# An encoder block on one core: another order of its opening, low parts of four output weights on another engine, and one pair of loads ahead of another

## The chip, the cores and the metric

The kernel runs on one NeuronCore of a Trainium2 chip. The metric is the device time of one execution in microseconds (us). Five engines work beside each other, each through its own list of instructions, in order: PE (TensorE: matrix products and transposes), DVE (VectorE), ACT (ScalarE), POOL (GpSimd) and SP (SyncE, which here only issues DMAs). They wait for each other through semaphores.

## The reference, cut to what matters

All tensors are float32; 1024 tokens, 1024 features.

```
h = LN_in(x)
p = h @ W_in                      # 1024 x 11776: q/k/v of 3 dilated attention groups,
                                  # HGRN2 query, two forget gates, input, output gate, two merge gates
a = dilated_attention(p)          # 512 wide
r = bidirectional_HGRN2(p)        # 1024 wide
m = sigmoid(g_a) * (a @ W_a) + sigmoid(g_r) * (r @ W_r)
h = LN1(alpha * h + m @ W_o)
h = LN2(alpha * h + SwiGLU(h))    # W_ffn_in 1024 x 5632, W_ffn_out 2816 x 1024
```

## The kernel before, in words

Every large matrix product keeps float32 precision by splitting both operands: a high part `hi` is a rounded copy (a cast on ACT), the low part `lo = x - hi` is a subtraction, and each product is three matmuls, hi*hi, hi*lo and lo*hi (`mm3`). `split` (L202) makes such a pair; its last argument says whether POOL or DVE subtracts.

On top of that the products of W_in and W_ffn_in are Strassen-Winograd products of a two by two block scheme: seven products take the place of eight. For W_in the activations are cut into two halves of 512 tokens (tiles 0 to 3, tiles 4 to 7 of 128 tokens) and two halves of 512 features. The blocks are called b11 (features 0 to 511 of the first four tiles), b21 (features 512 to 1023 of the same), b12 and b22 (the same of the last four tiles). The right operands of the seven products are b11, b21, b22 and the four sums t1 = b12 - b11, t2 = b22 - t1, t3 = b22 - b12 and t4 = b21 - t2 (before forms t4 as b21 - b11 - t3, the same thing). They are kept, as hi and lo, in `xb`. The left operands are blocks of weights a11, a12, a21, a22 and their sums s1 to s4. `ORDER = (1, 2, 6, 5, 7, 3, 4)` is the order of the products: product 1 uses b11, 2 uses b21, 6 uses t2, 5 uses t1, 7 uses t3, 3 uses b22, 4 uses t4. One product is twelve 128x512 matmuls.

`phase0` (L306) makes `xb`: for each tile of 128 tokens it loads x, takes mean and variance on DVE, normalises on ACT, stores the normalised tile to DRAM (`ah_d`, for the residual later), transposes on PE (`transposed`, L280), scales and shifts the transposed pieces out of PSUM on ACT or DVE, and splits them. Tiles are taken whole, one after the other.

`stream` (L473) is a generator that does W_in's products: groups `n` of four 128-wide column tiles, two pairs `g` in a group, and for each group the seven products for both pairs. It loads the weight blocks (`block`, L460), splits each three products ahead (`prep`), and passes each result to an evacuation on ACT or DVE. `phase1` runs it; attention and HGRN2 units run beside it as generators, on PE in between and on the other engines, and near the end `residual` (L364) loads the normalised tiles back, scales them with alpha and stores them for LN1.

`phase2` does W_a, W_r and W_o. W_o is held whole as hi and lo in two halves, `wo[0]` and `wo[1]` (`wo1hi`, `wo1lo` in the trace), made of eight chunks of 128 columns by `wo_chunk` (L1166) from two staging buffers. It ends with LN1, the blocks b11 to t4 of the next scheme, of which b22, t3 and t4 go to DRAM (`td`). `ffn_in` loads those back (`t_raw`, L1471), in the order b22, t3, t4, while the first products of W_ffn_in run; `ffn_raws` (L1405) loads the next weights. `ffn_out` and LN2 end the kernel.

Instructions are put in order per engine by a scheduler that follows the order of writing and priorities; `ordered` and `behind` add an order between two instructions, without a semaphore where they are on one engine.

Of the kernel before, what the change touches and what calls it, by code (L numbers as in the profile page):

```python
# [10 lines left out]
F32 = mybir.dt.float32  # L11
# [63 lines left out]
CST_PAD = 160  # L75
# [4 lines left out]
class Block:  # L80
    evac_ahead = 1000

    def __init__(self, ctx, tc, x, ln_in_g, ln_in_b, w_in, hgrn_lb, hgrn_norm_g, w_att_up, w_hgrn_up,
# [28 lines left out]
        self.ah_d = scratch("ah", 8)  # L112
# [25 lines left out]
    def consts(self):  # L138
# [20 lines left out]
        self.my = take(64).bitcast(I32)  # L159
        self.mhalf = cst.tile([128, 8], F32, name="mhalf")  # L160
        nc.vector.memset(self.mhalf, -0.5)

    def columns(self, pool):

        nc = self.nc
        rows = pool.tile([128, 128], F32, name="vrows")
        at, r = {}, 0
        for name, src, n in (("gin", self.ln["in"][0], 8), ("bin", self.ln["in"][1], 8), ("g1", self.ln["1"][0], 8),
                             ("b1", self.ln["1"][1], 8), ("lb", self.lbw, 32), ("ng", self.ng, 1)):
            nc.scalar.dma_start(rows[r:r + n, :], bass.AP(tensor=src.tensor, offset=src.offset, ap=[[128, n], [1, 128]]))  # L170
            at[name] = r
            r += n
        ps = self.ps_sd()
        nc.tensor.transpose(ps[:, :r], rows[:r, :], self.ident[:r, :r])
        a, b = self.cst.tile([128, 32], F32, name="vc"), self.cst1.tile([128, 33], F32, name="vc1")
        nc.vector.tensor_copy(a, ps[:, 0:32])
        nc.vector.tensor_copy(b, ps[:, 32:65])
        self.col = {n: a[:, at[n]:at[n] + 8] for n in ("gin", "bin", "g1", "b1")}
        self.lbraw, self.ngraw = b[:, 0:32], b[:, 32:33]

# [21 lines left out]
    def split(self, hi, lo, src, eng_hi="act", eng_lo="pool", key=None):  # L202
        nc = self.nc
        if eng_hi == "act":
            nc.scalar.copy(hi, src)  # L205
        else:
            nc.vector.tensor_copy(hi, src)
        e = nc.gpsimd if eng_lo == "pool" else nc.vector
        ins = e.tensor_sub(lo, src, hi.bitcast(F32))  # L209
        if key:  # L210
            self.ordered(key, ins)

# [14 lines left out]
    def behind(self, ins):  # L227

        if self.gone is not None:
            self.tc.add_manual_dep(ins.ins, self.gone, mybir.DependencyInfo(  # L230
                mybir.DependencyClass.NoSync, mybir.DependencyReason.DATA), reason="order behind an evacuation")
# [21 lines left out]
    def mm3(self, ps, whi, wlo, xhi, xlo, first, last, **kw):  # L253
# [3 lines left out]
        nc.tensor.matmul(ps, wlo, xhi, start=False, stop=last, **kw)  # L257
# [22 lines left out]
    def transposed(self, pool, n, q, g, b, v=None, bufs=2, on_act=(1, 3, 6)):  # L280

        nc = self.nc
        ps = self.ps_sd()
        for k in range(4):
            nc.tensor.transpose(ps[:, 128 * k:128 * (k + 1)], n[:, 128 * (4 * q + k):128 * (4 * q + k + 1)],
                                self.ident)
        if v is None:
            v = pool.tile([128, 4, 128], F32, name="tsv", tag="tsv", bufs=bufs)
        for k in range(4):
            kk = 4 * q + k  # L290
            p = ps[:, 128 * k:128 * (k + 1)]
# [6 lines left out]
    def phase0(self, pool):  # L298


        nc, kept, rest = self.nc, [], []

        def hold(n):
            t = pool.tile([128, D], F32, name=n, tag="xt", bufs=7)
            return t, [t[:, HALF * i:HALF * (i + 1)].rearrange("p (k c) -> p k c", k=4) for i in range(2)]

        xs = []

        def load():
            tt = len(xs)  # L310
            if tt < 8:
                xs.append(hold("xt"))
                for h in range(2 if tt == 0 else 1):
                    s = slice(HALF * h, HALF * (h + 1)) if tt == 0 else slice(0, D)
                    nc.sync.dma_start(xs[tt][0][:, s], self.x[128 * tt:128 * (tt + 1), s])

        for tt in range(8):
            for _ in range(4 if tt == 0 else 1):
                load()
            xt, (t1, t2) = xs[tt]  # L320
            if tt == 0:
                self.columns(pool)
                gc, bc = self.col["gin"], self.col["bin"]
            if tt == 1:
                self.rest()
            mv = self.stats(pool, xt, "0")
            self.normalise(pool, xt, xt, mv)
            nc.scalar.dma_start(self.ah_d[tt], xt)
            c = slice(128 * (tt % 4), 128 * (tt % 4) + 128)

            def put(name, v, c=c):
                hi, lo = self.xb[name]
                self.split(hi[:, :, c], lo[:, :, c], v, eng_lo="dve")

            if tt < 4:
                v = [self.half3("v11"), self.half3("v21") if tt == 0 else
                     pool.tile([128, 4, 128], F32, name=f"v21{tt}")]
                kept.append(v)
                for q, n in enumerate(("b11", "b21")):
                    self.transposed(pool, xt, q, gc, bc, v[q], on_act=(1, 3, 4, 6))  # L340
                    put(n, v[q])
                yield
                continue
            b11, b21 = kept[tt - 4]
            _, (b12, b22) = hold("vt")
            self.transposed(pool, xt, 0, gc, bc, b12, on_act=(0, 1, 3))
            nc.vector.tensor_sub(t1, b12, b11)
            put("t1", t1)
            self.transposed(pool, xt, 1, gc, bc, b22, on_act=(4, 5, 7))
            nc.vector.tensor_sub(t2, b22, t1)  # L350
            put("t2", t2)
            rest.append((put, b12, b22, b21, b11))

        for put, b12, b22, b21, b11 in rest:
            nc.vector.tensor_sub(b12, b22, b12)
            put("t3", b12)
        for put, b12, b22, b21, b11 in rest:
            put("b22", b22)
# [1384 lines left out]
```

## Time and profile before

| what | us |
|---|---|
| three runs: lowest, median, highest | 2112.54, 2115.25, 2120.56 |
| the profiled execution | 2111.09 |
| its span from first to last instruction | 2109.3 |
| PE busy in the span | 2022.3 |
| DVE, ACT, POOL busy | 1373.2, 925.0, 1087.2 |

PE is busy for 96% of the span, the others for half to two thirds. The span and what lies around it (1.8 us) make the profiled execution's time. In the listings below a row has start, duration, engine, source line, operation, output <- inputs, and in brackets the idle time before it with what ended it. Matmuls overlap, so the distance of two starts is what one of them costs, not its duration.

### The profile page before, as it was taken

To read this page: it belongs to the slowest core of one execution; us is meant where nothing else is said; L and a number is where in the kernel's file an instruction comes from. 1 tells how busy PE (TensorE), PEld (TensorE's weight loads), DVE (VectorE), ACT (ScalarE), POOL (GpSimd) and SP (SyncE) were. 2 spreads that over 40 slices of the span, in tenths; PEclk is the share of its full clock that TensorE was granted. 3 is DMA by queue.
4 is the path that set the end of the run, shared out by engine and by line. 5 is a ranking of instruction groups with operands and counts; after the bars stand their busy time and mean duration, and the time that the engine had idled before them with its cause. 6 is when DMAs were issued, how large, how long until landed. Compare 5 with 4: busy or idle time off the path is not lost.

```text
span 2109.3 us, 30917 instructions
## 1 busy us (share of the span) xinstructions
PE 2022.3 (96%) x10973; PEld 1673.1 (79%) x10973; DVE 1373.2 (65%) x2168; ACT 925.0 (44%) x1872; POOL 1087.2 (52%) x886
## 2 busy tenths in 40 slices
PE   4799999999999999999999999999999999999998
PEld 3678788888887888887888788788788888887876
DVE  7667745786459754788444823347867677767778
ACT  6544455444554435644355331144433333344542
POOL 3466654567446764565634864343666566630012
PEclk9899999999999999999999999999999999999999
DMA  5333442435333443343434764344434344348423
GB/s 204 110 129 100 138 159 93 142 129 168 121 105 126 135 154 120 125 131 115 157 117 143 279 222 142 98 136 134 155 120 147 129 148 136 113 161 296 160 90 125
DMA packets 273884, 301.10 MB, mean 143 GB/s; under 512 B 14081, under 2 KB 205378, under 8 KB 273730
## 3 DMA queue, kind: packets, MB, share of 16 engines
q1 hardware_dynamic: 266272, 273.73, 40.0%
q10 hardware_dynamic: 7458, 25.40, 3.1%
q8 instruction: 86, 1.41, 0.3%
q14 instruction: 68, 0.56, 0.1%
HBM read 200.25 MB, written 98.83 MB: 142 GB/s over the span
## 4 chain that ended last, share of the span: by engine, by line
PE 78%; DVE 10%; issue 5%; POOL 3%; DMA 2%; ACT 1%; SPq 0%; DVEq 0%; ACTq 0%; POOLq 0%
PE pj L255 17%; PE pj L256 17%; PE pj L257 17%; PE sd L255 6%; PE sd L256 6%; PE sd L257 6%; PE sd L1055 2%; POOL w_lo L209 2%; DVE qd L970 1%; DVE hR L1016 1%; DVE qd L973 1%; PE sd L811 1%; PE sd L860 1%; PE sd L887 1%; DVE hR L1015 1%
## 5 line engine op out<-in xcount | busy, mean ns | idle before, releaser
L209 POOL TENSOR_TENSOR w_lo<-wa,w_hi 128x512 fp32r<-128x512 f32 x276 | 382.2, 1392 | 301.0 <-ACT w_hi L205 271.0
L205 ACT CAST w_hi<-wa 128x512 fp32r<-128x512 f32 x276 | 170.0, 618 | 261.4 <-PE pj L256 169.3
L209 POOL TENSOR_TENSOR w_lo<-wsum,w_hi 128x512 fp32r<-128x512 f32 x88 | 128.7, 1472 | 112.7 <-PE sd L257 60.7
L200 POOL TENSOR_TENSOR mv<-mv,mhalf 128x1 f32<-128x1 f32 x24 | 15.4, 647 | 226.0 <-DVE mv L199 222.9
L209 POOL TENSOR_TENSOR w_lo<-f_raw,w_hi 128x512 fp32r<-128x512 f32 x66 | 102.0, 1554 | 55.8 <-ACT w_hi L205 54.6
L255 PE MATMUL pj<-xt1hi,w_hi 128*128 128x512 f32 x260 | 104.7, 403 | 17.4 <-ACT xt1hi L205 10.7
L205 ACT CAST w_hi<-wsum 128x512 fp32r<-128x512 f32 x88 | 54.8, 622 | 124.3 <-PE sd L256 114.8
L257 PE MATMUL pj<-xt1hi,w_lo 128*128 128x512 f32 x260 | 102.6, 395 | 1.0 <-POOL w_lo L209 1.0
L256 PE MATMUL pj<-xt1lo,w_hi 128*128 128x512 f32 x260 | 102.9, 396 | 0.0
L255 PE MATMUL pj<-xb22hi,w_hi 128*128 128x512 f32 x260 | 102.5, 394 | 0.0
L257 PE MATMUL pj<-xb22hi,w_lo 128*128 128x512 f32 x260 | 101.6, 391 | 0.0
L256 PE MATMUL pj<-xb22lo,w_hi 128*128 128x512 f32 x260 | 101.5, 390 | 0.0
L511 ACT COPY wkeep<-pj 128x512 f32<-128x512 f32 x138 | 80.1, 581 | 36.5 <-DVE evh L430 13.1
L209 POOL TENSOR_TENSOR w_lo<-ws,w_hi 128x512 fp32r<-128x512 f32 x46 | 64.5, 1406 | 60.9 <-ACT w_hi L205 58.8
L205 ACT CAST gwsum<-a_raw 128x512 fp32r<-128x512 f32 (+1 forms) x78 | 47.6, 615 | 100.2 <-PE pj L256 45.5
L403 DVE TENSOR_TENSOR evh<-wkeep,pj 128x512 f32<-128x512 f32 x66 | 57.6, 879 | 50.2 <-PE pj L257 35.4
L414 DVE TENSOR_TENSOR evh<-wkeep,pj 128x512 f32<-128x512 f32 x48 | 32.8, 683 | 88.0 <-PE pj L257 70.5
L489 POOL TENSOR_TENSOR wa<-wa,wa 128x512 f32<-128x512 f32 x46 | 68.2, 1492 | 31.8 <-DVE ws L488 29.8
L209 DVE TENSOR_TENSOR gwkeep<-a_raw,gwsum 128x512 fp32r<-128x512 f32 (+1 forms) x78 | 57.8, 742 | 40.5 <-ACT gwsum L205 37.6
L255 PE MATMUL pj<-xt2hi,w_hi 128*128 128x512 f32 x192 | 77.9, 407 | 2.6 <-ACT xt2hi L205 1.8
L255 PE MATMUL pj<-xb11hi,w_hi 128*128 128x512 f32 x192 | 77.4, 404 | 2.7 <-DVE evh L414 1.5
L257 PE MATMUL pj<-xt2hi,w_lo 128*128 128x512 f32 x192 | 76.0, 396 | 2.4 <-POOL w_lo L209 2.4
(407 smaller groups left out, 6572.2 us busy)
## 6 DMA issues: line engine op xcount, KB each, us to landing
wa<-in_w_in_dram SPq DMA_DIRECT2D x184, 256.0 KB, 3.2
f_raw<-in_w_ffn_in_dram SPq DMA_DIRECT2D x44, 512.0 KB, 4.1
a_raw<-gd SPq DMA_DIRECT2D x30, 512.0 KB, 3.7
gd<-fc SPq DMA_DIRECT2D x44, 256.0 KB, 2.0
gd<-fs SPq DMA_DIRECT2D x33, 256.0 KB, 2.1
tg<-evh SPq DMA_DIRECT2D x32, 256.0 KB, 3.3
tg<-tg SPq DMA_DIRECT2D x16, 512.0 KB, 3.5
y<-ahs SPq DMA_DIRECT2D x16, 512.0 KB, 4.7
```

The costliest lines, as they stand in the source:

```text
L205: nc.scalar.copy(hi, src)
L209: ins = e.tensor_sub(lo, src, hi.bitcast(F32))
L255: nc.tensor.matmul(ps, whi, xhi, start=first, stop=False, **kw)
L256: nc.tensor.matmul(ps, whi, xlo, start=False, stop=False, **kw)
L257: nc.tensor.matmul(ps, wlo, xhi, start=False, stop=last, **kw)
L403: self.left(nc.vector.tensor_tensor(o, self.order_src(add, g, kind), s, OP.add))
L414: self.left(nc.vector.tensor_add(t, add, ps))
L489: nc.gpsimd.tensor_sub(a["a21"], a["a11"], a["a21"])
L511: nc.scalar.copy(t, ps)
L811: nc.tensor.matmul(ps[:, tt % 2, :], q[pb, 128 * tt - 64:128 * tt + 64], k[pb, 128 * (tt - 1):128 * (tt + 1)], start=True, stop=True)
L860: nc.tensor.transpose(ps[:, o:o + 128], tile(tt, hd)[:, e:e + 128], ident)
L1055: nc.tensor.matmul(po[:, jj, :], l, r, start=(n == 0), stop=(n == len(terms) - 1))
```

## The change

Three places are edited; the functions for the near attention (`att_near`) are the same, line for line, in both kernels.

**The opening.** `phase0` first brings only b11 of tiles 0 to 3 to its end, then b21 of the same tiles, then tiles 4 to 7. The statistics' small steps go to POOL (an add, the power -0.5, and the shift) and stay in `mv0`; a half tile is normalised at a time; transposed pieces of a half tile leave PSUM on one engine, mostly, from one bank; t4 is b21 - t2 and t3 is subtracted on POOL. The normalised tile is no longer stored: `residual` loads x again and normalises it once more on ACT. The columns of parameters come in two parts, and loads are issued in a given order.

`stream` starts with product 1 of group 0 and group 1, then product 2 of both, and only then the other five of group 0, the other five of group 1, and all seven of each group that follows. Four explicit gates order casts and transposes behind others.

```
+        order = [(n, (p,)) for p in O[:2] for n in (0, 1)]
+        order += [(n, O[2:] if n < 2 else O) for n in range(len(tiles) // 4)]
...
+        def norm(tt, q):
+            x, mv = xs[tt][0][:, HALF * q:HALF * (q + 1)], self.mv0[:, tt, :]
+            ins = nc.scalar.activation(x, x, AF.Identity, bias=mv[:, 3:4], scale=mv[:, 2:3])
...
+        norm(3, 0)
+        turn(3, 0, v[3][0], (2, 3))
+        put(3, "b11", v[3][0])
+        self.gates = [at["hi", 1, "b11"]] * 2 + [at["hi", 3, "b11"]] * 2
+        run(2)
+        for tt in range(4):
+            if tt < 3:
+                norm(tt + 1, 1)
+            turn(tt, 1, v[tt][1], DVE if tt % 2 else ACT, self.product)
+            self.left(put(tt, "b21", v[tt][1]))
...
-            nc.sync.dma_start(a, self.ah_d[tt])
+            nc.sync.dma_start(a, self.x[128 * tt:128 * (tt + 1), :])
+            mv = self.mv0[:, tt, :]
+            nc.scalar.activation(a, a, AF.Identity, bias=mv[:, 3:4], scale=mv[:, 2:3])
```

On DVE this is what stands in the middle of the opening of the kernel before, while tiles 0 to 3 are made (`v_282` is tile 0's first half, `v_283` its second; `v_320` and `v_321` are tile 1's, `v_356` and `v_357` tile 2's, `v_392` tile 3's first).

```order
L295 TENSOR_SCALAR v_392<-sd,vc 128x128
L209 TENSOR_TENSOR xb21lo<-v_283,xb21hi 128x4x128
L488 TENSOR_TENSOR ws_690<-wa_428,wa_430 128x512
L360 TENSOR_TENSOR v_283<-v_283,v_282 128x512
L209 TENSOR_TENSOR xb11lo<-v_282,xb11hi 128x4x128
L295 TENSOR_SCALAR v_356<-sd,vc 128x128
L295 TENSOR_SCALAR v_357<-sd,vc 128x128
L209 TENSOR_TENSOR xb21lo<-v_321,xb21hi 128x4x128
L490 TENSOR_TENSOR wa_424<-ws_690,wa_424 128x512
```

Low parts of b11 and b21, sums of weights and differences for t4 stand mixed there. In the changed kernel the same engine has this, from the last low part of b11 on (`v_284`, `v_282`, `v_288`, `v_286` are the second halves of tiles 1, 0, 3, 2; `bn_453` and `bn_569` are the statistics of tiles 4 and 5):

```order
L220 TENSOR_TENSOR xb11lo<-v_287,xb11hi 128x4x128
L336 BN_STATS bn_453<-xt 128x6 x2
L336 BN_STATS bn_569<-xt 128x6 x2
L340 BN_AGGR mv_203<-bn_453 128x2
L340 BN_AGGR mv_203<-bn_569 128x2
L312 TENSOR_SCALAR v_284<-sd,vc 128x128 x4
L312 TENSOR_SCALAR v_288<-sd,vc 128x128 x4
L220 TENSOR_TENSOR xb21lo<-v_284,xb21hi 128x4x128
L220 TENSOR_TENSOR xb21lo<-v_282,xb21hi 128x4x128
L220 TENSOR_TENSOR xb21lo<-v_288,xb21hi 128x4x128
L605 TENSOR_TENSOR ws_504<-wa_273,wa_277 128x512
L605 TENSOR_TENSOR ws_529<-wa_275,wa_279 128x512
```

All of b11 is ahead of all of b21, and the statistics of the later tiles and the sums of weights have moved behind b11.

**Low parts of W_o's second half.** `wo_chunk` gets an argument, and chunks 4 to 7 are subtracted on DVE instead of POOL.

```
-    def wo_chunk(self, hl, c):
+    def wo_chunk(self, hl, c, by="pool"):
...
-        self.split(hi[:, :, s], lo[:, :, s], raw)
+        self.split(hi[:, :, s], lo[:, :, s], raw, eng_lo=by)
...
-                self.wo_chunk(wo[1], c)
+                self.wo_chunk(wo[1], c, "dve")
```

On DVE they stand here now, between the last evacuation of W_r (`mT`, L1319) and the first ones of W_o (`y`, L1372); the four of them are gone from POOL, where they stood in one piece.

```order
L1318 SCALAR_TENSOR_TENSOR tg<-tg,pj 128x512
L1319 TENSOR_TENSOR mT_11984<-mT_11984,tg 128x512
L220 TENSOR_TENSOR wo1lo<-w_raw,wo1hi 128x8x128 x2
L1372 SCALAR_TENSOR_TENSOR y_12901<-pj,y_12901 128x512
L199 BN_STATS bn_12995<-y_12901 128x6
L220 TENSOR_TENSOR wo1lo<-w_raw,wo1hi 128x8x128 x2
L1372 SCALAR_TENSOR_TENSOR y_12941<-pj,y_12941 128x512
```

Two of them now follow the first evacuation of W_o.

**b22's loads.** The weights of the fourth W_ffn_in group are ordered behind the last load of b22.

```
+                    if i == 0:
+                        b22_load = ins.ins.name
...
-                    nxt = self.ffn_raws(f + 1)
+                    nxt = self.ffn_raws(f + 1, after=b22_load if f == 2 else None)
```

On SP's queue before, `td_199`, `td_200` and `td_201` being b22, t3 and t4 in DRAM:

```order
L1314 DMA td_200<-tsum 512x1x128
L1314 DMA td_201<-tsum 512x1x128
L1409 DMA f_raw<-in_w_ffn_in_dram 128x8x128
L1471 DMA t_raw<-td_199 128x1024 x2
L1471 DMA t_raw<-td_200 128x1024 x2
L1409 DMA f_raw<-in_w_ffn_in_dram 128x8x128
```

and in the changed kernel, where they are `td_191`, `td_192` and `td_193`:

```order
L1417 DMA td_192<-tsum 512x1x128
L1417 DMA td_193<-tsum 512x1x128
L1576 DMA t_raw<-td_191 128x1024 x2
L1576 DMA t_raw<-td_192 128x1024 x2
L1512 DMA f_raw<-in_w_ffn_in_dram 128x8x128 x2
L1576 DMA t_raw<-td_193 128x1024 x2
```

One load of weights has moved from ahead of b22's two loads to behind t3's; all of them still stand behind the stores of t3 and t4.

More of the change, by code (lines that the diff above doesn't have):

```diff
@@ new lines, in turn, with run, late @@
+        def turn(tt, q, dst, act, gate=None):
+            gc, bc = self.col["gin"], self.col["bin"]
+            return self.transposed(pool, xs[tt][0], q, gc, bc, dst, on_act=[4 * q + k for k in act], two=len(act) == 2,
+                                   gate=gate)
+        ACT, DVE = range(4), ()
+        def run(n=1):
+            for _ in range(n):
+                next(work)
+        def late(tt, i):
+            put(tt, ("t1", "t3", "b22", "t4")[i], v[tt][i])
+        cols = self.columns(pool)
@@ new lines, in phase0 @@
+        load(4)
+        next(cols)
+        run(2)
+        load(2)
+        run()
+        for tt in range(4):
+            v[tt] = self.half3("v11"), self.half3("v21") if tt == 0 else                 pool.tile([128, 4, 128], F32, name=f"v21{tt}")
+        stats(0)
+        next(cols)
+        next(cols)
+        norm(0, 0)
+        norm(0, 1)
+        turn(0, 0, v[0][0], DVE)
+        stats(1)
+        put(0, "b11", v[0][0], "pool")
+        norm(1, 0)
+        stats(2)
+        turn(1, 0, v[1][0], ACT)
```

296 lines of the change are left out of this document (175 added, 121 removed).

## The prediction

> **What bounds the kernel now.** I read the page first, then the busy times in the opening, then the timelines of PE and of what it waits for at the three places that the change touches.
>
> ```profile
> PE 2022.3 (96%) x10973; PEld 1673.1 (79%) x10973; DVE 1373.2 (65%) x2168; ACT 925.0 (44%) x1872; POOL 1087.2 (52%) x886
> ```
>
> PE sets the time: 2022.3 of 2109.3 us. The change leaves all products and matmuls as they are, so it can gain only what PE idles, 87.0 us, and what it loses by running slowly behind an idle stretch. Where those lie, the busy times of two stretches show (time, length, then PE's busy time and instructions):
>
> ```profile
> 0.00:38.00 38.00, 11.58 (x42) 7.85 (x43) 26.60 (x73) 21.46 (x38) 14.50 (x26) 1.00 0.78 269
> 38.00:98.00 60.00, 47.11 (x194) 37.00 (x194) 40.63 (x70) 35.65 (x71) 21.88 (x19) 0.89 0.24 74
> ```
>
> 26.4 us are idle before 38 and 12.9 in the next 60, where the granted clock is 0.89. So 39 of the 87 us fall into the opening, which the change rewrites. PE's timeline there (start, duration, instruction, idle time before it):
>
> ```profile
> 37.63 1.22 PE L255 MATMUL pj<-xb11hi,w_hi 128*128 128x512 f32 x2
> ...
> 41.71 0.63 PE L257 MATMUL pj<-xb11hi,w_lo 128*128 128x512 f32 x1
> 42.14 0.63 PE L255 MATMUL pj<-xb11hi,w_hi 128*128 128x512 f32 x1
> ...
> 66.20 1.22 PE L255 MATMUL pj<-xt1hi,w_hi 128*128 128x512 f32 x2 [10.70 <-ACT xt1hi L205]
> 69.21 1.22 PE L255 MATMUL pj<-xt2hi,w_hi 128*128 128x512 f32 x2 [1.78 <-ACT xt2hi L205]
> ...
> 97.52 0.39 PE L257 MATMUL pj<-xt4hi,w_lo 128*128 128x512 f32 x1
> 97.75 0.39 PE L255 MATMUL pj<-xb11hi,w_hi 128*128 128x512 f32 x1
> ```
>
> The first product begins at 37.63. Four products (1 and 2 of group 0, two pairs) are all that PE can do without t1 and t2, and then it stands 10.70 us, and 1.78 more. Behind such a gap a matmul takes 0.43 us (41.71 to 42.14), later 0.23 (97.52 to 97.75). At 0.227 us, twelve matmuls make a product of 2.73 us. Group 0's 14 products are over at 97.75, of which they need 38.2: the opening costs PE **59.5 us** beside its products. With group 1's 14 products 97.75 becomes 135.9. That is the number to set against the change.
>
> **The opening, step by step.** Operations first, from DVE and ACT:
>
> ```profile
> 8.00 1.29 DVE L191 BATCH_NORM_STATS2 bn<-xt 128x6 f32<-128x512 f32 x2 [2.08 <-DMA xt<-in_x_dram]
> ...
> 12.31 1.23 DVE L191 BATCH_NORM_STATS2 bn<-xt 128x6 f32<-128x512 f32 x2
> ```
> ```profile
> 19.57 0.73 DVE L295 TENSOR_SCALAR v<-sd,vc 128x128 f32<-128x128 f32 x2 [2.46 <-ACT v L293]
> ```
> ```profile
> 65.41 0.68 DVE L209 TENSOR_TENSOR xt1lo<-xt,xt1hi 128x512 fp32r<-128x512 f32 x1
> 66.02 0.68 DVE L209 TENSOR_TENSOR xb22lo<-vt,xb22hi 128x512 fp32r<-128x512 f32 x1
> ...
> 71.43 0.68 DVE L209 TENSOR_TENSOR xt2lo<-xt,xt2hi 128x512 fp32r<-128x512 f32 x1
> ```
> ```profile
> 45.55 0.62 ACT L205 CAST w_hi<-wa 128x512 fp32r<-128x512 f32 x1 [1.31 <-PE pj L256]
> 46.07 0.58 ACT L511 COPY wkeep<-pj 128x512 f32<-128x512 f32 x1
> 46.55 0.46 ACT L293 ACTIVATE vt<-sd,vc 128x128 f32<-128x128 f32 x1
> 46.90 1.24 ACT L278 ACTIVATE xt<-xt,mv 128x1024 f32<-128x1024 f32 x1
> ```
>
> By distances of starts: DVE takes 1.44 us for a tile's statistics (three tiles in 8.00 to 12.31), 0.33 for one more 128x128 piece (two in 0.73), 0.60 for a 128x512 subtraction; ACT takes 0.52 for a cast, 0.35 for a piece, 1.24 for a whole tile.
>
> First b11 product: x1 to x3 land as before, so their statistics on DVE end at 12.3; then come 10 pieces (3.3) and three low parts (1.8), 17.4 without any wait. Walked through in the new order, each step behind what it waits for, the last low part is there at 19.9 and PE's first product begins near 19.5, 18 us earlier than 37.63. That alone is no gain: the gain is what PE does before t2. Products 1 and 2 of both groups are eight, 21.8 us, where four were ready. The first runs cold, about 4 us; PE has done all eight near **50** and waits for t2.
>
> t2 is DVE's to make. From 19.9 to the last xt2lo it has eight statistics instructions at 0.61 (4.9), 24 pieces (7.9) and 34 subtractions and sums of 128x512 (20.5): 33.3 us, so 53 if it never waits. Walked through with its waits for ACT's casts and PE's transposes I get 60.5. POOL can lengthen it:
>
> ```profile
> 48.68 1.54 DVE L209 TENSOR_TENSOR xt2lo<-xt,xt2hi 128x512 fp32r<-128x512 f32 x1 [0.16 <-ACT xt2hi L205]
> ```
> ```profile
> 46.30 3.38 POOL L209 TENSOR_TENSOR w_lo<-wa,w_hi 128x512 fp32r<-128x512 f32 x1 [3.48 <-ACT w_hi L205]
> ```
>
> Here 1.54 in place of 0.68 while POOL subtracts: 0.86 more. Three such meetings give 2.6, so **63**. From there 20 products (54.6) and 1.5 for the cold start end both groups at 119.1, against 135.9: **-17**. Bounds: t2 at 53 gives -27; t2 at 72, where the last xt2lo stands now (71.43), gives -8. I take 63, a walk through the list, between them. The stores of the normalised tiles vanish here; PE waits for none of them, so I count 0.
>
> **Low parts of wo[1].** PE, POOL, SP and ACT around its first use:
>
> ```profile
> 1368.61 0.39 PE L257 MATMUL pj<-wo0hi,w_lo 128*128 128x512 f32 x1
> 1370.68 0.73 PE L255 MATMUL pj<-wo1hi,w_hi 128*128 128x512 f32 x2 [1.69 <-ACT wo1hi L205]
> 1373.11 0.79 PE L256 MATMUL pj<-wo1lo,w_hi 128*128 128x512 f32 x1 [1.70 <-POOL wo1lo L209]
> ...
> 1376.27 0.42 PE L257 MATMUL pj<-wo1hi,w_lo 128*128 128x512 f32 x1
> ```
> ```profile
> 1360.32 4.75 POOL L209 TENSOR_TENSOR wo1lo<-w_raw,wo1hi 128x1024 fp32r<-128x1024 f32 x2
> ```
> ```profile
> 1362.74 2.75 SPq L1170 DMA_DIRECT2D w_raw<-in_w_o_dram  x2
> ```
> ```profile
> 1366.65 1.05 ACT L205 CAST wo1hi<-w_raw 128x1024 fp32r<-128x1024 f32 x1 [6.05 <-DMA w_raw<-in_w_o_dram]
> ```
> ```profile
> 1490.30 1.23 DVE L209 TENSOR_TENSOR xb22lo<-t_raw,xb22hi 128x1024 fp32r<-128x1024 f32 x1 [2.40 <-ACT xb22hi L205]
> ...
> 1493.31 2.31 DVE L209 TENSOR_TENSOR xb22lo<-t_raw,xb22hi 128x1024 fp32r<-128x1024 f32 x1
> ```
>
> PE is ready at 1368.84 and reaches 1376.27 with nine matmuls (2.04 us) in 7.43: **5.4 lost**, all that can be had. The third and fourth chunk are loaded into staging buffers that POOL frees, at 2.38 us each. DVE needs 1.23 for this shape (2.31 beside POOL). Then buffers come free near 1361.0 and 1362.2, the loads start 1.7 and 2.8 earlier, ACT casts at 1366.0 and 1367.8, and the low parts end near 1367.2 and 1369.0, about when PE asks. Behind them on DVE wait mT and y, one subtraction late at most. I take **-4.5**; bounds -5.4 and 0 (DVE held up by PE's evacuations so that nothing is early).
>
> The Trainium skill, "GPSIMD Engine Reference", section "1. Specifications", says that POOL shares its SBUF interface with DVE instructions that have two SBUF inputs. The rows with 2.31 and 1.23 agree. By that rule four meetings would cost DVE 9.2 instead of 4.9 and the gain would be about 1.
>
> **b22's loads first.**
>
> ```profile
> 1486.02 0.39 PE L257 MATMUL pj<-xt2hi,w_lo 128*128 128x512 f32 x1
> 1490.32 1.32 PE L255 MATMUL sd<-xb22hi,w_hi 128*128 128x512 f32 x2 [3.91 <-ACT xb22hi L205]
> ...
> 1496.61 0.39 PE L256 MATMUL sd<-xb22lo,w_hi 128*128 128x512 f32 x1
> ```
> ```profile
> 1482.16 0.58 SPq L1409 DMA_DIRECT2D f_raw<-in_w_ffn_in_dram  x1
> 1482.85 2.31 SPq L1471 DMA_DIRECT2D t_raw<-td  x4
> ```
> ```profile
> 1489.22 1.04 ACT L205 CAST xb22hi<-t_raw 128x1024 fp32r<-128x1024 f32 x1 [4.43 <-DMA t_raw<-td]
> ```
>
> From 1486.25 to 1496.61 PE does 15 matmuls (3.4 us) in 10.4: 7.0 lost. One weight load stands on SP ahead of t_raw; without it t_raw is issued 0.65 us earlier and doesn't share the DMA engines with 512 KB of weights. It lands 6.4 us after its issue now; by my estimate the cast starts near 1486.8, 2.4 earlier. The weights behind it are for products a group later. I take **-2.5**: the wait gets shorter, the cold stretch after it stays. Bounds: -0.6 (the issue alone) and -5 (the wait is too short to cool PE).
>
> The Trainium skill, "TensorE: Matmul & The Clock Gate", section "HAM oscillation — how this bites in real kernels", has the clock fall behind idle gaps over some 3.4 us. By that rule the shorter wait would leave PE warm, and this term would be -5. The trace speaks against it: behind gaps of only 1.69 and 1.70 us the matmuls at 1373.71 and after take 0.63.
>
> **The residual** has a term on the other side. Eight normalisations of 128x1024 go to ACT at 1.24 us (9.9 us of ACT), among the products of W_in, each behind a load of x:
>
> ```profile
> DMA to landing us min/median/max: 2.6/4.7/7.1
> ```
>
> That is how long the same-sized loads from ah took there. Casts of weights stand behind them on ACT, three products (8.2 us) ahead of PE. ACT is busy 44%, so it has some 4.6 us to spare in 8.2, and 1.24 fits. With a load that is late now and then I take **+1.5**; bounds 0 and +5.
>
> The near attention is the same in both kernels: 0, since it has no edited line.
>
> **Sum:** -17 - 4.5 - 2.5 + 1.5 = -22.5, on the profiled execution's 2111.1: 2088.6. That execution lies 4.2 below the median of 2115.25 and 1.5 below the lowest run; on the median the sum is 2092.7. I forecast **2090**.
>
> **The rivals.**
>
> *t2 stays as late as now.* Pieces, statistics and weights' sums all sit on DVE ahead of the last xt2lo, and ACT's queue can hold DVE: the fifth cast of weights waits for the first product to free its buffer, and the normalisations of tiles 4 and 5 stand behind it. Then the opening gives 8 or less: 2098 to 2106. For it speaks that 53 is without a single wait; against it that the wait of 10.70 falls in a stretch where DVE is busy 40.63 of 60. Chance 0.17.
>
> *The small edits do nothing.* wo1 is late anyway and t_raw lands by DMA share, not order: -17 - 0.6 + 1.5 gives 2095. Chance 0.12.
>
> *t2 comes at 53.* DVE never waits: -27 in the opening, 2078. Chance 0.06.
>
> *Slower: the residual stops ACT.* If ACT waits the whole landing time for x, each tile costs 7.1 + 1.24 - 4.6 = 3.7 us of PE, eight of them 30, and -24 + 30 gives 2117. It decides from a wait of 6.4 us at each load (6.4 + 1.24 - 4.6 = 3.0, eight times 24). Against it: the loads are issued by SP well ahead, in four buffers. Chance 0.07.
>
> **How the numbers follow.** The forecast's own band, 2080 to 2097, has 0.58. About 0.5% (10.6 us, so 2104.7) is what a measurement of this kernel can tell from no change. Forecast, small edits, t2 at 53 and nearly half of the first rival lie below: 0.84 faster; the rest of the first rival and a little of the last give 0.10 the same; 0.06 slower. The range must hold t2 at 53 with all small terms (2111 - 27 - 5.4 - 5 + 1.5 = 2075) and t2 at 72 with none (2111 - 8 + 1.5 + 2 = 2107), so 2072 to 2108.
>
> **What would show it.** Right: first xb11 matmul at 19 to 22; eight products without a long gap until near 50; first xt2 product with its low part at 60 to 65; the last xt4 product of group 1 near 119; no wait for wo1lo and under 1 us for wo1hi; wait for xb22hi near 1.5 us; ACT's wait for x in the residual near 0. Wrong: xt2lo after 70, PE idle over 15 us between products 2 and 6, w_hi named in PE's waits near 1150 to 1210, or the four wo1lo at over 2 us on DVE.

## The result and the profile after

The changed kernel takes **2099.26 us** in the median of four runs (2098.61 to 2102.44), the kernel before 2116.36 in four (2112.54 to 2120.56): a ratio of 0.9922 with a 95% interval of 0.99 to 0.9944, so 12 to 21 us less. 2090 was forecast, in a range of 2072 to 2108: faster as said, by 17.1 us (8.65 between the two profiled executions, 2111.09 and 2102.44) instead of some 25. The time lies above the forecast's own band of 2080 to 2097, inside the range. The profiled execution of the changed kernel has a span of 2100.6 us. From its page, PE:

```profile
PE 2025.1 (96%) x10974; PEld 1675.0 (80%) x10974; DVE 1380.4 (66%) x2158; ACT 931.8 (44%) x1878; POOL 1093.8 (52%) x903
```

PE idles 75.5 us instead of 87.0. The same two stretches as before (time, length, then the busy time of PE, PE's weight loads, DVE, ACT, POOL):

```profile
0.00:38.00 38.00, 21.21 (x91) 15.84 (x91) 23.24 (x48) 26.51 (x51) 20.69 (x40) 1.00 0.65 200
38.00:98.00 60.00, 44.52 (x184) 35.09 (x185) 47.97 (x85) 31.59 (x62) 33.28 (x30) 0.83 0.23 75
```

PE has 21.2 us of work in the first 38 us, where it had 11.6. In the next 60 it has less than before, 44.5 instead of 47.1, and DVE has more, 48.0 instead of 40.6. PE's timeline says why:

```profile
19.48 1.65 PE L268 MATMUL pj<-xb11hi,w_hi 128*128 128x512 f32 x3 [2.31 <-ACT xb11hi L212]
...
53.70 0.39 PE L270 MATMUL sd<-xb21hi,w_lo 128*128 128x512 f32 x1
54.90 0.66 PE L300 MATMUL sd<-tabs_sb,xt 128*128 128x128 f32 x4 [0.81 <-ACT xt L347]
57.20 0.91 PE L300 MATMUL sd<-tabs_sb,xt 128*128 128x128 f32 x4 [1.65 <-DVE evh L495]
68.94 1.22 PE L268 MATMUL pj<-xt2hi,w_hi 128*128 128x512 f32 x2 [10.83 <-ACT xt2hi L212]
70.57 0.79 PE L269 MATMUL pj<-xt2lo,w_hi 128*128 128x512 f32 x1 [0.41 <-DVE xt2lo L220]
...
128.87 0.39 PE L268 MATMUL pj<-xb11hi,w_hi 128*128 128x512 f32 x1
```

The first product starts at 19.48 and all eight that need only b11 and b21 are done at 53.9. Then PE stands 10.83 us for t2, about as long as it stood for t1 before (10.70, and 1.78 more for t2), but with eight products behind it and not four. Group 2 begins at 128.87. In the kernel before:

```profile
141.85 0.39 PE L255 MATMUL pj<-xb11hi,w_hi 128*128 128x512 f32 x1
```

So 13.0 us are won by then. Further on the lead (how much earlier the changed kernel is at the same work) changes: it is 6.3 us at group 21's first product (1134.31 against 1140.6), 8.5 behind W_o and 9.7 after b22.

### The profile page after: what moved, and what is told of

Read it like the earlier page. It is cut to its first block, busy times and chain, and to the rows that moved or that the text cites. A ratio compares the mean times of both kernels' runs of the same rounds, so it can differ in the third digit from the quotient of the medians.

```text
span 2100.6 us, 30922 instructions
## 1 busy us (share of the span) xinstructions
PE 2025.1 (96%) x10974; PEld 1675.0 (80%) x10974; DVE 1380.4 (66%) x2158; ACT 931.8 (44%) x1878; POOL 1093.8 (52%) x903
## 4 chain that ended last, share of the span: by engine, by line
PE 79%; DVE 9%; issue 5%; POOL 3%; DMA 3%; ACT 1%; SPq 0%; ACTq 0%; DVEq 0%; POOLq 0%
PE pj L268 17%; PE pj L270 17%; PE pj L269 17%; PE sd L269 6%; PE sd L268 6%; PE sd L270 6%; PE sd L1164 2%; POOL w_lo L220 2%; DVE qd L1079 1%; PE sd L920 1%; PE sd L969 1%; PE sd L996 1%; PE sd L1113 1%; DVE hR L1125 1%; PE sd L696 1%
## 5 line engine op out<-in xcount | busy, mean ns | idle before, releaser
L220 POOL TENSOR_TENSOR w_lo<-wa,w_hi 128x512 fp32r<-128x512 f32 x272 | 377.1, 1394 | 290.6 <-ACT w_hi L212 258.9
L208 POOL TENSOR_TENSOR mv<-mv,mhalf 128x1 f32<-128x1 f32 x16 | 10.8, 679 | 208.2 <-DVE mv L207 208.0
L1116 ACT ACTIVATE hS<-hR,dec 128x128 f32<-128x128 f32 x112 | 44.4, 402 | 76.7 <-DVE hR L1125 46.9
```

What stands on the lines that cost most here:

```text
L1116: nc.scalar.activation(S[:, c, :], E, AF.Copy, scale=dec[:, 1, c:c + 1])
```

## Experiments

"The changed kernel" is the one above. A median is set against the medians of the kernel before in the runs beside it (2113.96 to 2114.66). An effect on the opening is best read in the trace, as the distance from PE's first b11 matmul to its first t2 matmul, since the first matmul itself wanders between 18.6 and 20.2. That distance is 49.46 in the changed kernel.

**The changed kernel again, no edit (after_again).**

> The changed kernel once more, unedited, as the base of the other runs of this chip and for a second trace: time 2096 to 2101; the stretch from group 2's first product to group 21's, 5.4 us longer than before in one pair of traces, comes out 2 to 4 us longer if single cold stretches of PE between executions made up the rest.

Measured: 2100.83 against 2114.66, ratio 0.9938 (0.9924 to 0.9952): 13.8 us less, where the first pair had 17.1. The distance is 49.96, and the stretch from group 2 to group 21 takes 1005.4 us, as in the first trace (1005.4); 2 to 4 us above the 998.8 of the kernel before, 1001 to 1003, were expected. So the longer middle isn't one odd execution; more on it below. What follows for the rest: two medians of the same kernel lie 3 us apart in their lead, and a total that differs by less tells nothing.

**Only the opening and the residual (small_undone).**

```
-                self.wo_chunk(wo[1], c, "dve")
+                self.wo_chunk(wo[1], c)
...
-                    nxt = self.ffn_raws(f + 1, after=b22_load if f == 2 else None)
+                    nxt = self.ffn_raws(f + 1, after=None)
```

> The changed kernel with wo[1]'s low parts on POOL and b22's loads in the order of before, so the opening (with the residual) alone. If the terms add up: 4.7 to 7 us above the changed kernel, 2104 to 2106, and 9 to 12 us below before. Rival (opening gains little and the small edits carry the result): above 2109.

Measured: 2106.47, ratio 0.9958 (0.9946 to 0.997): 8.2 us below before (9 to 12 were expected) and 5.6 above after_again, and the rival, above 2109, falls. The old waits are back, 2.00 and 1.70 us for wo[1], 4.38 for b22:

```profile
1364.24 0.73 PE L268 MATMUL pj<-wo1hi,w_hi 128*128 128x512 f32 x2 [2.00 <-ACT wo1hi L212]
1366.67 0.80 PE L269 MATMUL pj<-wo1lo,w_hi 128*128 128x512 f32 x1 [1.70 <-POOL wo1lo L220]
...
1485.19 1.32 PE L268 MATMUL sd<-xb22hi,w_hi 128*128 128x512 f32 x2 [4.38 <-ACT xb22hi L212]
```

**Only the small edits (before_small)**: the kernel before, with the two edits above added.

> The kernel before with only the two small edits: the low parts of wo[1]'s chunks on DVE, b22's loads ahead of the weights. If the small terms are what the two profiles show at their places (-4.7 and -1.2), the time is 5.9 below before, about 2109, ratio 0.9972; no wait for wo1lo and a wait for xb22hi under 2.5 us. Rival: they came from the shifted times of everything in the changed kernel, and alone give under 2 us.

Measured: 2109.16 against 2113.96, ratio 0.9978 (0.9969 to 0.9986), 4.8 us less where 5.9 was expected. PE's timeline where it takes up wo[1] and b22:

```profile
1374.96 0.50 PE L257 MATMUL pj<-wo1lo,w_hi 128*128 128x512 f32 x1 [0.37 <-DVE wo1lo L209]
...
1488.69 1.02 PE L256 MATMUL sd<-xb22hi,w_hi 128*128 128x512 f32 x2 [1.94 <-ACT xb22hi L205]
1489.95 0.50 PE L257 MATMUL sd<-xb22lo,w_hi 128*128 128x512 f32 x1 [0.24 <-DVE xb22lo L209]
1490.28 0.39 PE L258 MATMUL sd<-xb22hi,w_lo 128*128 128x512 f32 x1
```

Both waits shrink without the new opening, and the rival falls. The parts add up: 8.2 from the opening with the residual and 4.8 from the small edits make 13.0, beside 13.8 in after_again.

**Products in the old order (group0_first)**: b11 first as in the changed kernel, but group 0's seven products before group 1's. The blocks of group 1 that come early go with it, and the points at which the opening lets products and sums of weights run are set back too.

```
-        order = [(n, (p,)) for p in O[:2] for n in (0, 1)]
-        order += [(n, O[2:] if n < 2 else O) for n in range(len(tiles) // 4)]
+        order = [(n, O) for n in range(len(tiles) // 4)]
```

> The opening brings b11 first as the changed kernel does, but the products stand as before: all seven of group 0, then group 1. If the gain comes from the four more products that are ready before t2, they are lost: PE waits 10.9 us more for t2 (about 21 to 22 in place of 10.8), group 2's first product comes near 139 to 140 and the time is 2108 to 2111. Rival (the earlier b11 and the earlier t2 are the gain, and the order of the products only moves the wait): group 2 near 129 to 132, time 2099 to 2102.

Measured: 2108.14, ratio 0.9969 (0.9957 to 0.998), 6.2 us below before instead of 14 to 17. Group 2 begins at 136.26:

```profile
65.92 0.79 PE L268 MATMUL pj<-xt2hi,w_hi 128*128 128x512 f32 x1 [8.62 <-ACT xt2hi L212]
```
```profile
136.26 0.39 PE L268 MATMUL pj<-xb11hi,w_hi 128*128 128x512 f32 x1
```

7.4 us later than in the changed kernel, less than the 10.9 of four products, because t2 comes 3 us earlier (distance 46.12): DVE has three instructions with two inputs fewer ahead of it (34 instead of 37 up to the last xt2lo), and PE's shorter list of products lets tiles through sooner; which of these does it was not tried. The wait for t2 is not one of 21 us either: PE stands 2.84, 5.48 and 5.98 us on the way to it. The four more products are most of the opening's gain, 7.4 of 13.0: that theory holds, its number (10.9) was 3.5 us too large.

**Why is t2 late? t3 and t4 behind it (t3t4_late).** The prediction had t2 at 63 and it came at 69. Theory 1: DVE's list, stretched where POOL works beside it. Theory 2: a chain through tile buffers and banks.

```
-            nc.gpsimd.tensor_sub(b12, b22, b12)
-            nc.vector.tensor_sub(b21, b21, t2)
...
+            if i == 1:
+                self.behind(nc.vector.tensor_sub(v[tt][1], v[tt][2], v[tt][1]), at["lo", 7, "t2"])
+            if i == 3:
+                self.behind(nc.vector.tensor_sub(v[tt][3], v[tt][3], v[tt][4]), at["lo", 7, "t2"])
+                nc.vector.tensor_sub(v[tt][3], v[tt][3], v[tt][1])
```

> t3's and t4's subtractions both behind the last xt2lo, on DVE. Theory 1: the last xt2lo 6 to 8 us earlier, at 62 to 64, and the time 4 to 7 us below the changed kernel's 2099, 2092 to 2095, as the moved subtractions fit before t3 and t4 are asked for. Theory 2: xt2lo at 68 or later, time 2099.

What stands on DVE ahead in the changed kernel, and on POOL beside it:

```profile
56.38 0.67 DVE L495 TENSOR_TENSOR evh<-wkeep,sd 128x512 f32<-128x512 f32 x1
...
61.64 0.69 DVE L426 TENSOR_TENSOR xt<-vt,xt 128x512 f32<-128x512 f32 x1
62.37 1.64 DVE L429 TENSOR_TENSOR v<-v,xt 128x512 f32<-128x512 f32 x1
63.93 0.68 DVE L220 TENSOR_TENSOR xt2lo<-xt,xt2hi 128x512 fp32r<-128x512 f32 x1
...
68.27 1.65 DVE L429 TENSOR_TENSOR v<-v,xt 128x512 f32<-128x512 f32 x1
69.84 0.68 DVE L220 TENSOR_TENSOR xt2lo<-xt,xt2hi 128x512 fp32r<-128x512 f32 x1
```
```profile
56.14 1.45 POOL L220 TENSOR_TENSOR w_lo<-ws,w_hi 128x512 fp32r<-128x512 f32 x1 [2.03 <-ACT w_hi L212]
61.69 1.77 POOL L428 TENSOR_TENSOR vt<-vt 128x512 f32<-128x512 f32 x1 [4.10 <-DVE xt L422]
67.56 1.81 POOL L428 TENSOR_TENSOR vt<-vt 128x512 f32<-128x512 f32 x1 [4.10 <-DVE xt L422]
```

And in this kernel:

```profile
62.64 0.69 DVE L220 TENSOR_TENSOR xt2lo<-xt,xt2hi 128x512 fp32r<-128x512 f32 x1 [0.68 <-ACT xt2hi L212]
67.65 0.69 DVE L220 TENSOR_TENSOR xt2lo<-xt,xt2hi 128x512 fp32r<-128x512 f32 x1 [0.68 <-ACT xt2hi L212]
```

The last xt2lo comes 2.2 us earlier, the distance to t2 falls by 1.6 to 47.83. From b11 to the last xt2lo DVE has four subtractions fewer and works 5.2 us less on those with two inputs (24.0 instead of 29.2), but its waits and its other work, which is the same, take 22.9 us instead of 20.2: 2.7 of the 5.2 reappear as waits, two of them the 0.68 for the cast of t2 above. Neither theory has its number: by this DVE's list and the chain through ACT and the buffers are nearly equally long. The time is 2103.23, ratio 0.9953 (0.9939 to 0.9968), not better: PE waits 3.19 us for POOL's w_lo at 117, where the changed kernel has no such wait over 0.63 between t2 and group 2. That the longer t4 delays the weights was not tried by itself.

**t3 alone behind t2 (t3_late)**: `self.behind(nc.gpsimd.tensor_sub(...), at["hi", 7, "t2"])` on POOL. The order has no semaphore between engines, so POOL ran two of the four earlier than meant, at 57.41, beside DVE's low part of t1 and the sums for product 3.

> t3's subtraction stays on POOL but behind the last cast of t2; DVE's instructions ahead of the last xt2lo are the same. Theory 1 with meetings of DVE and POOL as the price: the four t4 subtractions fall from 1.67 us towards 0.7, and the last xt2lo comes 3 to 4 us earlier, near 66. If the meetings cost nothing on the path: 0 to 1 us. Theory 2: 0.

Measured, DVE and then POOL:

```profile
56.84 2.83 DVE L611 TENSOR_TENSOR wa<-wa,wa 128x512 f32<-128x512 f32 x2
59.59 1.75 DVE L220 TENSOR_TENSOR xt1lo<-xt,xt1hi 128x512 fp32r<-128x512 f32 x1
```
```profile
57.41 3.38 POOL L374 TENSOR_TENSOR vt<-vt 128x512 f32<-128x512 f32 x2
```

The two sums take 2.83 (1.75 in the changed kernel) and xt1lo 1.75 (0.68). t2 comes 1.7 us later, PE waits 12.79, and the one time is 2104.2. The edit missed its aim, but it shows the price on the path: from tile 5's xt2lo to tile 7's DVE has the same instructions, 2.2 us more of such meetings with POOL, and takes 16.2 us instead of 14.1. (Ahead of that it was 0.4 quicker, so t2 is 1.7 later.) It is one execution, read in its trace.

**t4 alone behind t2 (t4_late)**: the t4 lines of t3t4_late alone.

> t4's subtraction is moved behind the last low part of t2 (as b21 - b11 - t3, two subtractions in place of one). In the changed kernel DVE's four t4 subtractions take 6.7 us ahead of the last xt2lo (69.84), and 35 subtractions with two inputs take 32 us there instead of 21. Theory 1 (DVE's length, stretched by POOL, sets t2): the last xt2lo comes 5 to 7 us earlier, at 63 to 65, and group 2's first product near 123 to 124 instead of 128.87. Theory 2 (tiles 6 and 7 wait in a chain for tile buffers and for PSUM banks): xt2lo moves by 0 to 2 us.

This one execution was granted a clock of 0.655 from end to end and took 2893.54 us; nothing in it is compared.

**A seventh buffer (xt7)**: `tag="xt", bufs=7` in place of 6, paid for with `tag="wfirst", bufs=1` in place of 3.

> Seven buffers for the tiles of the opening instead of six, so that the pieces of tiles 6 and 7 don't wait for the low part of t1 of tiles 4 and 5 (the room comes from the first weight blocks of group 1, which get one buffer instead of three). Theory 2 (the chain through the buffers sets t2): last xt2lo 4 to 6 us earlier than 69.84, at 64 to 66, and the time 2094 to 2096. Theory 1 (the length of DVE's list, stretched by POOL): DVE has the same work ahead of it, so 68 to 70, time 2098 to 2100. A third: with one buffer the blocks of group 1 come late and PE waits for w_hi between products; then the time is above 2100.

Measured: last xt2lo at 69.44, distance 48.99, time 2101.32, ratio 0.9936 (0.9924 to 0.9949). DVE's first and last xt2lo, and ACT where the one weight buffer shows:

```profile
52.89 0.68 DVE L220 TENSOR_TENSOR xt2lo<-xt,xt2hi 128x512 fp32r<-128x512 f32 x1
...
69.44 0.68 DVE L220 TENSOR_TENSOR xt2lo<-xt,xt2hi 128x512 fp32r<-128x512 f32 x1
```
```profile
46.28 0.62 ACT L212 CAST w_hi<-wfirst 128x512 fp32r<-128x512 f32 x1 [4.78 <-DMA wfirst<-in_w_in_dram]
```

From tile 4's xt2lo to tile 7's it is 16.6 us instead of 19.5 (50.30 to 69.84), but that is not a price of the buffers alone: DVE waited only 0.6 of the 19.5 us. Most of the rest of the 3 us is that two instructions with two inputs now stand ahead of tile 4's xt2lo and that POOL costs DVE 0.9 less behind it. Tile 4 comes 2.6 later, behind ACT's wait of 4.78 for the late weight block. From b11 to the last xt2lo the 34 instructions with two inputs take 27.0 us instead of 29.2, and other work and waits 21.9 instead of 20.2: most of what was saved on meetings came back as waits. PE itself waits for no w_hi before group 2, so the third theory isn't borne out as it was put.

**Sums for product 3 behind t2 (sums_late).**

```
-            put(tt, "t2", t2)
+            ins = put(tt, "t2", t2)
+            if tt == 7:
+                self.left(ins)
```

> The changed kernel with the two weight sums for product 3 behind the last xt2lo on DVE, nothing else. Theory 1 (DVE's list, in its order, sets t2): they take 1.8 to 2.8 us ahead of tile 5's low part of t1, so the last xt2lo comes 1.8 to 2.8 us earlier than 69.84, at 67 to 68, and the time 2 us below the changed kernel's. Theory 2 (buffers and banks alone): no change over 0.5 us.

Measured: 2097.31, ratio 0.9923 (0.991 to 0.9936); last xt2lo at 69.75, with the first b11 matmul at 20.20, and so a distance of 48.66, 0.8 less than in the changed kernel (1.3 against after_again). Theory 1 had 1.8 to 2.8, theory 2 at most 0.5; as the distance differs by 0.5 between two traces of the changed kernel, this decides little. The lead of 17.4 us is that of the changed kernel's first runs (17.1), and the interval overlaps with after_again's.

**Both, a seventh buffer and the sums (xt7_sums_late).**

> As with seven buffers, and besides the two weight sums for product 3 (1.75 us on DVE ahead of tile 5's low part of t1 in the changed kernel) stand behind the last xt2lo. Theory 1: 2 to 3 us off the list, last xt2lo at 66 to 67. Theory 2: as with seven buffers alone, 64 to 66, and 1 us more at most. Both: 62 to 64 and time 2092 to 2095.

Measured: 2096.63, ratio 0.9925 (0.9911 to 0.9938); last xt2lo 67.45, distance 47.76, 1.7 earlier. Theory 1 had 66 to 67 for this, theory 2 at most 66 and both together 62 to 64: the result lies nearest to theory 1, with the late weight block in it, which neither had counted.

**Sums and the t4 of tiles 6 and 7 (sums_t4_late)**: as sums_late, and `nc.vector.tensor_sub(b21, b21, t2)` of those tiles in the later loop, behind the last xt2lo.

> The sums late and the t4 subtractions of tiles 6 and 7 (1.64 us each, no added work) behind the last xt2lo too. Theory 1, with the cast of t2's high part (0.68) coming out behind the t4 that covered it: 1.8 + 2 x 1.0 = 3.8 earlier, last xt2lo near 66, time 3 to 4 us below the changed kernel's, 2095. If the moved work makes the casts of later weights late, the gain is given back and the time is the changed kernel's within 1 us.

Measured: distance 48.41, 1.1 earlier instead of 3.8; 2100.53, ratio 0.9928 (0.9916 to 0.9939). The time is the changed kernel's, as the second case had it. Behind tile 4's xt2lo DVE now waits 1.9 us instead of 0.6, and the last two xt2lo take 0.99 instead of 0.68, beside POOL. No edit that keeps the order of the products brought t2 more than 2 us nearer, and no version here beats the changed kernel beyond the intervals.

**The residual from stored tiles (res_stored).**

```
+            if q == 1:
+                nc.scalar.dma_start(self.ah_d[tt], xs[tt][0])
...
-            nc.sync.dma_start(a, self.x[128 * tt:128 * (tt + 1), :])
-            mv = self.mv0[:, tt, :]
-            nc.scalar.activation(a, a, AF.Identity, bias=mv[:, 3:4], scale=mv[:, 2:3])
+            nc.sync.dma_start(a, self.ah_d[tt])
```

> The changed kernel, but the normalised tiles are stored in the opening and loaded by the residual as before, with no normalisation on ACT there. If the residual's normalisations cost what the two profiles show (about +2.5 between 1134 and the end of W_r), the stretch from group 21's first product to the last matmul of wo0 is 2 to 3 us shorter; the stores in the opening cost 0 to 1 us: time 2097 to 2099. Rival: the stores compete with the loads of x and of weights in the opening and move the first product from 19.5 to over 21; then the time is 2100 to 2103.

Measured: 2098.96, ratio 0.993 (0.9916 to 0.9943). The stretch from group 21's first product to the first wo[1] matmul, less the wait directly ahead of that, takes 229.05 us here and 230.7 in the changed kernel, 1.7 less where 2 to 3 were expected. Over all traces it is 229.0 with stored tiles (three, the two with the old opening among them: 228.4 to 229.6) and 230.5 with x (ten: 229.3 to 231.2). So 1.4 us in the mean for the normalisations, with single traces that overlap. The distance to t2 is 50.08, 0.1 to 0.6 more than in the two traces of the changed kernel, so the stores cost little, and the first product stays at 20.0: the rival falls. The total doesn't tell the two kernels apart.

## Why the prediction was right, and where its sizes failed

**First b11 product at 19.5: right.** It is 19.48, and 18.6 to 20.2 in the other traces. That it fits to 0.02 is luck: the last low part of b11, which was to be there at 19.9, ends at 21.1.

**Eight products by 50: 4 us off.** They end at 53.9. Waits of 1.37 and 1.35 for b21's parts, and one of 0.92 ahead of transposes, stand between them. As t2 was later still, this cost nothing.

**t2 at 63: wrong, and this is the step that failed.** The walk had 34 subtractions and sums at 0.60 (20.5 us), 12.8 us of other work and 7.4 of waits (60.5 against 53), and "three such meetings" with POOL (2.6); a meeting is a DVE instruction with two inputs that is longer because POOL works beside it. The trace has the same 34; other work and waits are 20.2 as in the walk, but the 34 take 29.2 us: **8.8** over their 20.4, not 2.6. The last xt2lo ends at 70.5 instead of 63.1. Of these 7.4 us, 6.2 are the meetings that were not counted, and 1.2 come from the start of the list, 21.1 instead of 19.9, where two low parts of b11 (17.80) take 3.33 us beside POOL, where two of b21 alone take 1.29. I took one meeting of before as if it were rare. In the changed kernel POOL subtracts t3 just while DVE subtracts t4 (1.64 beside 1.77, 1.65 beside 1.81), and low parts and sums of weights stand beside the rest. That meetings lengthen this path t3_late shows (2.2 us of them, 2.1 us of path), and from tile 4's xt2lo to tile 7's DVE waits for only 0.6 of 19.5 us. That they alone set it is not shown: t3t4_late took 2.8 us of them and 2.4 us of work away, and 2.7 came back as waits; in xt7 2.2 us of them were gone, and t2 came 0.5 nearer. Behind the list the chain of casts and buffers is nearly as long, and a price paid on DVE alone isn't a price of the path.

The Trainium skill, "GPSIMD Engine Reference", section "1. Specifications", has POOL share its SBUF interface with DVE instructions of two SBUF inputs. The trace agrees: of the 34, the ten that take over 0.75 us all have two inputs from SBUF and stand beside a step of POOL on 128x512, while `evh<-wkeep,sd`, of which one input is in PSUM (`sd`), takes 0.67 at 56.38 with POOL busy all along. Not each meeting is DVE's loss, either: the subtraction at 61.64 starts ahead of POOL's at 61.69 and keeps its 0.69, and POOL takes 1.77 in place of 1.29; the one at 62.37 starts inside POOL's and takes 1.64. The prediction weighed the rule at wo1lo, where it didn't bite, and took too little of it here, where it did.

**The opening, -17: right in kind, too large.** 13.0 us in the trace at group 2's start; 13.4 from the mean of two traces with the old opening (141.85, 143.30) to that of three with the new (128.87, 129.51, 129.29). 1.7 of them are not won: between group 2 and group 3 PE has 125 small operations beside the same 168 matmuls instead of 110, and takes 46.35 us instead of 44.66; 14 of the 15 more are work of HGRN2 that stood ahead of the mark before. That leaves some 11.5. The rest of that sum: PE resumed at 68.94 instead of 63 (+5.9), and took 59.9 instead of 56.1 us to group 2, while the kernel before took 44.1 instead of 38.2 for group 1. I had counted products alone. In the kernel before, the 5.9 left out are mostly 2.96 of waits and 22 small operations of 2.6; in the changed kernel the 3.8 are mostly matmuls that ran slowly for longer (3.7 us instead of the 1.5 counted for the cold start), 1.0 of waits and eight small operations of 0.8.

**wo[1], -4.5: right.** PE, DVE, SP and ACT after:

```profile
1364.79 0.39 PE L270 MATMUL pj<-wo0hi,w_lo 128*128 128x512 f32 x1
1365.02 0.63 PE L268 MATMUL pj<-wo1hi,w_hi 128*128 128x512 f32 x2
1366.11 0.50 PE L269 MATMUL pj<-wo1lo,w_hi 128*128 128x512 f32 x1 [0.46 <-DVE wo1lo L220]
1366.45 0.39 PE L270 MATMUL pj<-wo1hi,w_lo 128*128 128x512 f32 x1
```
```profile
1355.87 2.89 DVE L220 TENSOR_TENSOR wo1lo<-w_raw,wo1hi 128x1024 fp32r<-128x1024 f32 x2
```
```profile
1357.65 1.52 SPq L1273 DMA_DIRECT2D w_raw<-in_w_o_dram  x2
```
```profile
1362.04 1.05 ACT L212 CAST wo1hi<-w_raw 128x1024 fp32r<-128x1024 f32 x1 [5.25 <-DMA w_raw<-in_w_o_dram]
```

No wait for wo1hi, 0.46 for wo1lo, and PE stays at 0.23 a matmul. POOL has little to do there, so the four low parts cost 1.2 to 1.5 each, not 2.31. From the time PE is ready to the first product of W_ffn_in it is 83.2 us (87.9 before): -4.7. In some executions it is less: after_again still waits 1.32 for wo1hi and takes 86.5.

**b22, -2.5: right at the place, half given back.**

```profile
1477.50 0.39 PE L270 MATMUL pj<-xt2hi,w_lo 128*128 128x512 f32 x1
1479.60 1.02 PE L268 MATMUL sd<-xb22hi,w_hi 128*128 128x512 f32 x2 [1.71 <-ACT xb22hi L212]
1480.86 0.79 PE L269 MATMUL sd<-xb22lo,w_hi 128*128 128x512 f32 x1 [0.24 <-DVE xb22lo L220]
1481.45 0.63 PE L270 MATMUL sd<-xb22hi,w_lo 128*128 128x512 f32 x1
...
1485.48 0.39 PE L269 MATMUL sd<-xb22lo,w_hi 128*128 128x512 f32 x1
...
1497.56 0.50 PE L268 MATMUL sd<-xt4hi,w_hi 128*128 128x512 f32 x1 [1.25 <-DVE wkeep L1545]
```
```profile
1473.74 2.17 SPq L1576 DMA_DIRECT2D t_raw<-td  x4
```
```profile
1478.50 1.04 ACT L212 CAST xb22hi<-t_raw 128x1024 fp32r<-128x1024 f32 x1 [2.21 <-DMA t_raw<-td]
```

The cast starts 4.8 us after the issue instead of 6.4, and the 15 matmuls up to 1485.48 are through in 7.75 instead of 10.4: 2.6 won. The cold stretch stayed, as forecast. Then PE waits 1.25 for DVE's `wkeep`. That wait (with one for xt3lo 1.2 to 1.7 together) stands in each kernel with the edit that was looked at and in none without, and leaves -1.2 at the next group. In four of the eleven traces with the edit PE stays at 0.23 a matmul behind the wait, and the gain at the next group is 2.1 to 2.3 instead of 0.7 to 1.3; even then it is far from the bound of -5. What comes late next was the question I did not ask here.

**The residual, +1.5: right in size,** 1.4 over the traces, but by a mechanism that I had not priced, so the size is partly luck. From group 21 to the first wo[1] matmul PE idles as long with x as with stored tiles, 5.9 us in the changed kernel and in res_stored. But with x one of the waits is 4.34:

```profile
1191.80 0.80 PE L270 MATMUL pj<-xb21hi,w_lo 128*128 128x512 f32 x1 [4.34 <-POOL w_lo L220]
```

DVE and POOL ahead of it:

```profile
1174.25 1.25 DVE L453 SCALAR_TENSOR_TENSOR a<-a,ginb 128x1024 f32<-128x1024 f32 x1 [4.33 <-ACT a L452]
...
1184.41 2.88 DVE L605 TENSOR_TENSOR ws<-wa,wa 128x512 f32<-128x512 f32 x1
```
```profile
1187.37 2.18 POOL L606 TENSOR_TENSOR wa<-wa,wa 128x512 f32<-128x512 f32 x1 [0.62 <-DVE ws L605]
1189.51 5.17 POOL L220 TENSOR_TENSOR w_lo<-wa,w_hi 128x512 fp32r<-128x512 f32 x3
```

It stands, with 4.30 to 4.35 us, at the same place in each of the ten traces with x, and in none of the three with stored tiles, where no wait there is over 1.5. Behind it PE runs cold: the eleven matmuls from 1192.39 to 1196.66 start 0.43 apart, 2.2 us more than at 0.23. So the normalisations cost not more idle time but idle time in one piece.

How they gather it is a reading of this trace. Backwards: the low part that PE waits for stands on POOL behind a sum of weights; this waits for DVE's sum; and DVE, where the residual's steps stand ahead of that sum, had waited 4.33 us for ACT's normalised tile. But with stored tiles DVE waits 3.8 to 4.6 us there for the load, so that wait isn't the new one. New, in each of the ten, is one of 2.74 for ACT's second tile, some 26 us behind group 21's first product; that it is the cause was not tried. I had queued only ACT's own casts behind the new step. I had also misread the time of the loads: the row 2.6/4.7/7.1 counts the tile's stores in, and the loads of ah alone took 4.7/6.6/7.1 (those of x take 3.9/6.1/6.7). Busy times and the granted clock (the third number from the end) of 75 us around the residual, after and then before:

```profile
1140.00:1215.00 75.00, 69.09 (x291) 55.96 (x290) 49.58 (x39) 39.06 (x60) 55.87 (x30) 0.95 0.75 256
```
```profile
1146.00:1221.00 75.00, 69.76 (x301) 55.77 (x301) 50.43 (x41) 30.45 (x53) 53.83 (x30) 1.00 0.76 263
```

ACT has 8.6 us more to do there, nearly the 9.9 that were priced, and the clock is 0.95 instead of 1.00.

**Sum.** -11.5, -4.7, -1.2 and +1.4 make -16.0, between the 13.8 and the 17.1 of the two pairs of medians. The first pair of traces shows only 8.6: between groups 2 and 21 its kernel before is the quickest of the traces seen (998.8 us; 1001.1 in before_small) and the changed kernel among the slowest (1005.4; 1000.9 to 1005.5 over eleven traces of it and its variants). Beside the 1.7 of moved work this stretch varies by 2 to 5 us from trace to trace; whether the new order itself adds 1 or 2 us there stays open.

The rival that the small edits do nothing falls with the 4.8 us of before_small, and t2 at 53 was never near. The slower rival did not come: ACT waits at most 1.76 us for a load of x, never 6. The first rival came out in part, and in time more than the forecast did. t2 is as late as before (last xt2lo at 69.84, where the kernel before had it at 71.43; the sign "xt2lo after 70" is missed by 0.16), and 2099.3 and 2100.8, the medians, lie in its 2098 to 2106 and not in the forecast's own band. But the opening gains 13.0, not the rival's 8. The eight products ahead of the wait were in that sum already; what it lacked is that PE takes up t2 at 68.94 instead of 72 (3.1), and that the kernel before needs 5.9 us more for group 1 than was counted where the changed kernel needs 3.8 more (2.1).

## What to carry to other kernels

Where an engine waits for a long preparation, work that needs only its first half can be worth most of its length: eight products ahead of the wait instead of four, 10.9 us more of work, gave 7.4 us of the opening's gain. When a list of one engine is added up for a forecast, count its meetings with a neighbour on the same memory from the new order, not from the old trace. And behind each wait that is removed, look for the next one: the waits that came back in t3t4_late and in xt7, the `wkeep` behind b22. Where short waits gather into a long one, as in the residual, the matmuls behind it run slowly, and the sum of the waits doesn't show it.

## What was not expected of the hardware

How long PE may idle before its clock falls isn't set by the idle time alone. Behind a wait of 1.71 us for b22 (and 0.24) the next matmuls ran at 0.43 us from start to start for some 3 us; behind 1.94 (and 0.24) in before_small they ran at 0.23 from the second on. The Trainium skill, "TensorE: Matmul & The Clock Gate", section "HAM oscillation — how this bites in real kernels", puts the fall behind gaps of over some 3.4 us; these runs show it behind 1.7, and the measurement decides. Over the eleven traces with the b22 edit that wait is 1.59 to 2.17 us; seven run at 0.43 behind it, and four, with 1.75 to 1.94, at 0.23. What chooses between the two cases at one length the runs do not show.

One execution in this study (t4_late) was granted a mean clock of 0.655 over its whole span and took 2893.54 us; the other traces have 0.986 to 0.991.
